# A two-layer encoder on one core: attention outputs moved to another pool, one distance table, and a written order for TensorE in the mixer

## The chip, the cores and the metric

The kernel runs on one core of one Trainium2 chip. The metric is the device time of one execution in microseconds (us); the kernel before takes 1097.06 us, the median of 3 runs (1096.51 to 1097.66).

## What is computed

Two layers, each of three sub-layers on 256 tokens of 1024 channels: a SwiGLU FFN with 2816 hidden channels, a token mixer, and a second FFN. Every sub-layer normalises its input, scales and shifts it by numbers from a conditioning vector, and adds its gated output to the residual. The mixer is the part that the change touches:

```
proj = n @ w_in                         # qa, ka, va, qd, kd, vd
qa = rope(rms(qa)); ka = rope(rms(ka))  # branch A: 8 query heads, 2 key heads
oa = softmax(qa @ ka.T / 8) @ va
sc = qd @ kd.T / 8 - slope[h] * |i - j| # branch B: 4 heads, two maps each
od = rms((softmax(sc[0]) - lam * softmax(sc[1])) @ vd)
g  = sigmoid(n @ w_gate + b_gate)
y  = (g_a * (oa @ w_ba) + g_b * (od @ w_bb)) @ w_o
```

The slopes of the four heads are 2^-2, 2^-4, 2^-6 and 2^-8.

## The kernel before, in words

All matrix products run on TensorE in float32r. An operand is split into a high part and the rest, and a product is three: high by high, rest by high, high by rest (mm3, lines 85 to 88). Weights come as 1 MB units through SP's queue into four raw buffers; ScalarE casts a half unit to its high part (whi, line 328) and VectorE subtracts it (wlo, line 330), each half into a slot of a pool of 23 slots of 4 KB per partition (w4). The same stream holds the units of the conditioning matrices, which VectorE reduces (raw<-raw,cb, line 245) or accumulates (gacc, line 276). pump makes the next halves; done calls it when a weight is used up.

The mixer's opening stretch, the front, goes from the end of the projection kv to the first gating product gt (lines 1026 to 1054). Its parts in the order of the code: to_T turns qr and kr of token half 0 (tt: four 128x128 transposes of qr, one of kr), proj_T makes half of qd's products (48, called pt), to_T turns token half 1, the other 48 of qd, a_scores(0, 0) (sc, 12 products), 48 products of kd, a_scores(0, 1), the other 48 of kd, a_T(0, 0) (8 transposes of softmax probabilities p, called pt as well, line 875), 24 products for vd (pj), a_T(0, 1), a_scores(1, 0), 24 more of vd, a_pv (ot) and a_scores(1, 1). kr is made from the projection by a reduction (hms), a power on GpSimd (hr), the rotation (q) and a product with hr, on VectorE (lines 757 to 826). p is made by a maximum on VectorE (nmx), two exponentials on ScalarE (line 852), a reciprocal (rs) and a product: by ScalarE for key head 0 (line 864), by VectorE for key head 1 (line 866).

The code's order is not the engines' order: a scheduler places the instructions of each engine within the dependencies, and only where follow ties two instructions is their order fixed. So TensorE's order in the front differs from the code's, as shown below.

After the front come the gates gt, branch B's attention, and merge: the products of the branches' outputs oaH, oaL, odH, odL with w_ba and w_bb (yb, 48 in each of four calls), whose moving operand is the branch output, 256 columns. The branch outputs lie in slots of w4, at 128 modulo 256 bytes; the modulated input nh and nl, which is the moving operand of gate and up products (g, u), qd, kd and gt, lies at 64 modulo 256, through a 192-byte tile ahead of it. In the FFN the last product of a down step, 512 columns wide, is parted in 264 and 248 columns (down_mm's part) ahead of the gate and up products.

Of the kernel before, what the change touches and what calls it, by code (L numbers as in the profile page):

```python
# [19 lines left out]
P = 128  # L20
# [22 lines left out]
def trunk(tc, a):  # L43
    nc = tc.nc
    with (
# [38 lines left out]

        def mm3(out, Lh, Ll, Rh, Rl, start, stop):
            nc.tensor.matmul(out, Lh, Rh, start=start, stop=False, skip_group_check=True)  # L86
            nc.tensor.matmul(out, Ll, Rh, start=False, stop=False, skip_group_check=True)  # L87
            nc.tensor.matmul(out, Lh, Rl, start=False, stop=stop, skip_group_check=True)  # L88
# [26 lines left out]
        for hf in range(2):  # L115
            x = slice(hf * 512, (hf + 1) * 512)
            bank = gen("cb")
            cmm = nc.tensor.matmul(bank, ones[0:1, :], crow[hf], start=True, stop=True)
            cact = nc.scalar.activation(cb[:, x], bank, AF.Silu)
# [169 lines left out]
        def gate_bcast(l, s):  # L289
# [5 lines left out]
            for hf in range(2):  # L295
# [5 lines left out]
                nc.tensor.matmul(bank, onesr, gh, start=True, stop=False, skip_group_check=True)  # L301
                nc.tensor.matmul(bank, onesr, gl, start=False, stop=True, skip_group_check=True)
# [57 lines left out]
        class Norm:  # L360
# [37 lines left out]
            def transposes(self):  # L398
                self.banks = []
                for hf in range(2):  # L400
                    bank = gen("nt")
                    for i in range(4):
                        nc.tensor.transpose(bank[:, i * P:(i + 1) * P], self.xs[hf][:, i * P:(i + 1) * P], ident)
# [82 lines left out]
        HF = [slice(0, 512), slice(512, 1024)]  # L486


        def new_hT():
            return (op.tile([P, 2, S], F32R, tag="hh", bufs=3, name=nm("hh")),  # L490
                    op.tile([P, 2, S], F32R, tag="hl", bufs=3, name=nm("hl")))

        def tok_hi(bank, ncol, unit_of, nT, t):
# [4 lines left out]
            for k in range(NK):  # L498
# [3 lines left out]
                nc.tensor.matmul(bank, nh[:, k, tok], wh[:, x], start=k == 0, stop=False, skip_group_check=True)  # L502
                nc.tensor.matmul(bank, nh[:, k, tok], wl[:, x], start=False, stop=False, skip_group_check=True)

        def tok_lo(bank, ncol, unit_of, nT, t, last):
            nh, nl = nT
            tok = slice(t * P, (t + 1) * P)
            for k in range(NK):
                u, i, c = unit_of(k)
                wh, wl = half(u, i)  # L510
                nc.tensor.matmul(bank, nl[:, k, tok], wh[:, c:c + ncol], start=False, stop=k == NK - 1, skip_group_check=True)
# [37 lines left out]
        def first_T(hts):  # L549

            tb = gen("tb")
            for t in range(2):
                for c in range(2):
                    nc.tensor.transpose(tb[:, c * 256 + t * P:c * 256 + (t + 1) * P], hts[t][:, c * P:(c + 1) * P], ident)
# [6 lines left out]
        def ffn(i, nT, norm1, first, nT_next):  # L561
# [6 lines left out]
            def down_mm(idx, t, hf, last, y=slice(0, 512), part=False):  # L568
# [4 lines left out]
                for c in range(2):  # L573
                    x = slice(c * 512 + y.start, c * 512 + y.stop)
                    if part and c == 1:

                        for L, R in ((hh, wh), (hl, wh)):
                            nc.tensor.matmul(acc[t][hf], L[:, c, tok], R[:, x], start=False, stop=False, skip_group_check=True)
# [827 lines left out]
```

## Time and profile before

| | |
|---|---|
| median of 3 runs | 1097.06 us |
| the profiled execution | 1097.68 us |
| its span, first to last instruction | 1095.9 us |
| TensorE busy in the span | 1082.9 us, 99% |
| VectorE busy | 864.9 us, 79% |
| ScalarE busy | 593.1 us, 54% |

The span leaves out 1.78 us that lie around it. A matmul's duration in the profile overlaps the next one's, so the rate of a stretch is read as its length by its number of products. In the views PE is TensorE, DVE VectorE, ACT ScalarE, POOL GpSimd; the timeline gives start and duration of merged rows, the windows give busy time of each engine in a stretch.

### The profile page before, as it was taken

The page shows a single profiled execution, that of the slowest core. Times are in us where ns is not written, and L with a number is a line of the kernel's source. Part 1 is how long each engine was busy: PE and PEld are TensorE (multiplying, and loading weights), DVE is VectorE, ACT ScalarE, POOL GpSimd, SP SyncE. Part 2 cuts the span into 40 slices and gives each one's busy share as a digit, 9 for nine tenths or more (in the row PEclk, how much of TensorE's full clock was granted, in tenths as well). Part 3 has the DMA queues.
Part 4 walks back from the last instruction along what each step waited for, and adds up shares of the span by engine and source line. Part 5 has one row for each costly group of instructions (what it writes and reads, how often), then busy time and mean ns, then how long its engine had stood idle before and what let it go on. Part 6 is the DMA issues. An engine that isn't in the chain of part 4 may idle for free.

```text
span 1095.9 us, 19235 instructions
## 1 busy us (share of the span) xinstructions
PE 1082.9 (99%) x7796; PEld 998.8 (91%) x7796; DVE 864.9 (79%) x1388; ACT 593.1 (54%) x916; POOL 44.5 (4%) x52
## 2 busy tenths in 40 slices
PE   8999999999999999999999999999999999999997
PEld 6989999898999899999989999989889998999996
DVE  5998986899978798886589886569988779766543
ACT  5564483558664554535455545435776547444432
POOL 1000000220010000000000000004000000000000
PEclk9999999999999999999999999999999999999999
DMA  8998996368745299997449987543865454876501
GB/s 315 380 368 336 380 335 219 120 263 332 264 172 193 86 376 357 347 377 266 150 152 357 365 288 285 202 165 126 297 236 189 157 190 183 315 267 229 197 19 39
DMA packets 44889, 271.12 MB, mean 247 GB/s; under 512 B 5880, under 2 KB 6648, under 8 KB 14848
## 3 DMA queue, kind: packets, MB, share of 16 engines
q1 hardware_dynamic: 42340, 267.93, 66.1%
q10 hardware_dynamic: 2460, 1.96, 0.6%
q8 instruction: 61, 1.00, 0.3%
q14 instruction: 28, 0.23, 0.1%
HBM read 268.82 MB, written 1.05 MB: 246 GB/s over the span
## 4 chain that ended last, share of the span: by engine, by line
PE 94%; DVE 3%; ACT 1%; issue 1%; POOL 0%; POOLq 0%
PE dn L87 6%; PE dn L88 6%; PE dn L86 6%; PE u L86 6%; PE g L86 6%; PE u L87 6%; PE g L88 6%; PE g L87 6%; PE u L88 6%; PE gt L86 3%; PE gt L88 3%; PE gt L87 3%; PE g L1199 2%; PE u L1199 2%; PE yb L88 1%; PE yb L87 1%
## 5 line engine op out<-in xcount | busy, mean ns | idle before, releaser
L330 DVE TENSOR_TENSOR wlo<-raw,whi 128x1024 fp32r<-128x1024 f32 x364 | 436.9, 1220 | 133.7 <-PE u L87 44.6
L328 ACT CAST whi<-raw 128x1024 fp32r<-128x1024 f32 x364 | 374.0, 1052 | 226.4 <-PE u L88 83.7
L86 PE MATMUL u<-nh,whi 128*128 128x256 f32 x592 | 164.0, 277 | 0.0
L86 PE MATMUL g<-nh,whi 128*128 128x256 f32 x592 | 164.0, 277 | 0.0
L87 PE MATMUL u<-nh,wlo 128*128 128x256 f32 x592 | 163.7, 277 | 0.0
L88 PE MATMUL g<-nl,whi 128*128 128x256 f32 x592 | 163.7, 277 | 0.0
L87 PE MATMUL g<-nh,wlo 128*128 128x256 f32 x592 | 163.7, 277 | 0.0
L88 PE MATMUL u<-nl,whi 128*128 128x256 f32 x592 | 163.6, 276 | 0.0
L86 PE MATMUL dn<-whi,hh 128*128 128x512 f32 (+1 forms) x326 | 126.0, 387 | 0.0
L87 PE MATMUL dn<-whi,hl 128*128 128x512 f32 (+1 forms) x326 | 125.9, 386 | 0.0
L88 PE MATMUL dn<-wlo,hh 128*128 128x512 f32 (+1 forms) x326 | 125.8, 386 | 0.0
L86 PEld LDWEIGHTS g<-nh,whi 128*128 128x128 f32 x592 | 111.2, 188 | 0.3
L87 PEld LDWEIGHTS g<-nh,wlo 128*128 128x128 f32 x592 | 111.2, 188 | 0.2
L86 PEld LDWEIGHTS u<-nh,whi 128*128 128x128 f32 x592 | 111.2, 188 | 0.1
L87 PEld LDWEIGHTS u<-nh,wlo 128*128 128x128 f32 x592 | 111.3, 188 | 0.0
L88 PEld LDWEIGHTS u<-nl,whi 128*128 128x128 f32 x592 | 111.2, 188 | 0.2
L88 PEld LDWEIGHTS g<-nl,whi 128*128 128x128 f32 x592 | 111.2, 188 | 0.0
L245 DVE CUSTOM_DVE_ANT_0 raw<-raw,cb 128x1024 f32<-128x1024 f32 x80 | 95.5, 1217 | 1.1 <-DMA raw<-in_ada_t_dram 0.9
L86 PE MATMUL gt<-nh,whi 128*128 128x256 f32 x256 | 73.7, 288 | 0.0
L88 PEld LDWEIGHTS dn<-wlo,hh 128*128 128x128 f32 x326 | 61.2, 188 | 12.4
L87 PEld LDWEIGHTS dn<-whi,hl 128*128 128x128 f32 x326 | 61.3, 188 | 11.1 <-DVE hl L546 0.2
L86 PEld LDWEIGHTS dn<-whi,hh 128*128 128x128 f32 x326 | 61.3, 188 | 11.1
(227 smaller groups left out, 2051.9 us busy)
## 6 DMA issues: line engine op xcount, KB each, us to landing
raw<-in_w_gu_dram SPq DMA_DIRECT2D x79, 1024.0 KB, 5.5
raw<-in_w_d_dram SPq DMA_DIRECT2D x41, 1024.0 KB, 6.4
raw<-in_ada_t_dram SPq DMA_DIRECT2D x40, 1024.0 KB, 6.8
raw<-in_ada_g_dram SPq DMA_DIRECT2D x24, 1024.0 KB, 6.3
raw<-in_w_in_dram SPq DMA_DIRECT2D x16, 1024.0 KB, 5.0
raw<-in_w_gate_dram SPq DMA_DIRECT2D x16, 1024.0 KB, 4.9
raw<-in_ada_t_dram SPq DMA_DIRECT2D x16, 512.0 KB, 6.5
raw<-in_w_gu_dram SPq DMA_DIRECT2D x32, 256.0 KB, 6.1
```

The source lines that it names most:

```text
L86: nc.tensor.matmul(out, Lh, Rh, start=start, stop=False, skip_group_check=True)
L87: nc.tensor.matmul(out, Ll, Rh, start=False, stop=False, skip_group_check=True)
L88: nc.tensor.matmul(out, Lh, Rl, start=False, stop=stop, skip_group_check=True)
L245: queue("dve", nc.vector.tensor_tensor_reduce(r, r, cb, 1.0, 0.0, op0=ALU.mult, op1=ALU.add, accum_out=col[:, k:k + 1]))
L328: split[1] = nc.scalar.copy(hi, r)
L330: split[0] = nc.vector.tensor_tensor(lo, r, hi.bitcast(F32), op=ALU.subtract)
L1199: nc.tensor.matmul(bank[:, c * 256:(c + 1) * 256], W[:, w], N[:, k, :], start=x + y + k + c == 0, stop=y == 1 and k == NK - 1, skip_group_ ...
```

## The change

The branch outputs leave w4: they share four buffers of 1088 words with the FFN's split activations, which now lie both in one such buffer, and begin 48 words into it, which is 64 modulo 256 bytes. w4 keeps its 23 slots. Branch B's query is scaled by 1/8 divided by its head's slope when it is split, so that one table of negative distances serves all heads, and the exponential multiplies by the slope. The last product ahead of the first yb (gb) and ahead of the third merge's yb (wo) is parted in 264 and 248 columns. Last, every TensorE instruction goes through an object that ties it to the one before while it is on: it is on from the first to_T of the mixer to the end of the last merge, so TensorE runs the code's order there.

```diff
+        class Ordered:
+            on, last = False, None
+            def then(self, ins):
+                if self.on and self.last is not None:
+                    follow(ins, self.last)
+                self.last = ins
+                return ins
+            def matmul(self, *args, **kw):
+                return self.then(nc.tensor.matmul(*args, **kw))
+            def transpose(self, *args, **kw):
+                return self.then(nc.tensor.transpose(*args, **kw))
+        pe = Ordered()
...
-                nc.tensor.matmul(bank, onesr, gl, start=False, stop=True, skip_group_check=True)
+                for z in (slice(0, PART), slice(PART, 512)) if part and hf else (slice(0, 512),):
+                    pe.matmul(bank[:, z], onesr, gl[:, z], start=False, stop=True, skip_group_check=True)
...
         def new_hT():
-            return (op.tile([P, 2, S], F32R, tag="hh", bufs=3, name=nm("hh")),
-                    op.tile([P, 2, S], F32R, tag="hl", bufs=3, name=nm("hl")))
+            x = op.tile([P, 1088], F32R, tag="h", bufs=4, name=nm("hhl"))
+            return tuple(x[:, i * 512:(i + 1) * 512].rearrange("p (c x) -> p c x", c=2) for i in range(2))
...
-                mc["pen"] = const("pen", [P, 4, 2, S])
+                mc["pen"] = const("pen", [P, 2, S])
+                nc.scalar.mul(mc["pen"], d, -1.0)
...
+                        if name == "qd":
+                            for x in range(2):
+                                o = [d[:, 2 * b + x, :] for d in dst]
+                                f = mc["qs"][:, x:x + 1]
+                                nc.scalar.activation(o[0], v[:, x, :], AF.Identity, scale=f)
+                                nc.vector.scalar_tensor_tensor(o[1], v[:, x, :], f, o[0].bitcast(F32), op0=ALU.mult,
+                                                               op1=ALU.subtract)
+                            continue
...
+            def branch_out(name):
+                x = op.tile([P, 1088], F32R, tag="h", bufs=4, name=nm(name))
+                return x[:, 48:48 + 4 * S].rearrange("p (k x) -> p k x", k=4)
...
-                    st["oa"] = (slot("oaH", (P, 4, S), F32R), slot("oaL", (P, 4, S), F32R))
+                    st["oa"] = (branch_out("oaH"), branch_out("oaL"))
...
-                        nc.scalar.activation(x[:, y], x[:, y], AF.Exp, bias=bi[:, m:m + 1], scale=0.125, accum_out=sm[:, m:m + 1])
+                        nc.scalar.activation(x[:, y], x[:, y], AF.Exp, bias=bi[:, m:m + 1], scale=SLOPES[2 * pair + e], accum_out=sm[:, m:m + 1])
...
             st["qaT"] = pair("qaT")
+            pe.on = True
             to_T(st["qr"][0], st["qaT"], 0, 4)
...
-            gate_bcast(l, 1)
+            gate_bcast(l, 1, True)
...
+                    if part and i == 1:
+                        for L, R in ((0, wh), (1, wh)):
+                            pe.matmul(acc[t][hf], ms_[k][:, L, tok], R[:, x], start=False, stop=False, skip_group_check=True)
+                        for z in (slice(0, PART), slice(PART, 512)):
+                            pe.matmul(acc[t][hf][:, z], ms_[k][:, 0, tok], wl[:, 512 + z.start:512 + z.stop], start=False,
+                                             stop=False, skip_group_check=True)
+                        continue
...
-                wo(0, 1, hf, 2)
+                wo(0, 1, hf, 2, hf == 1)
             merge(2)
             merge(3)
-            free(4)
+            pe.on = False
```

TensorE at the start of layer 0's front, around the transpose of the first kr (tt is the bank it goes to, ident the identity, pt the bank of qd's products). Before:

```order
L87 MATMUL pt_2537<-nh_164,wlo_2432 128x256
L88 MATMUL pt_2537<-nl_165,whi_2431 128x256
L86 MATMUL pt_2537<-nh_164,whi_2431 128x256
L87 MATMUL pt_2537<-nh_164,wlo_2432 128x256
L787 MATMUL tt_2532<-ident,kr_2466 128x128
L88 MATMUL pt_2537<-nl_165,whi_2431 128x256
L86 MATMUL pt_2536<-nh_164,whi_2431 128x256
```

Now, at the same place:

```order
L97 MATMUL kv_2460<-whi_2134,nl_165 128x256 x4
L97 MATMUL kv_2460<-whi_2247,nl_165 128x256 x4
L100 MATMUL tt_2516<-ident,qr_2398 128x128 x4
L100 MATMUL tt_2523<-ident,kr_2457 128x128
L97 MATMUL pt_2527<-nh_164,whi_2290 128x256
L97 MATMUL pt_2527<-nh_164,wlo_2291 128x256
```

The transpose of kr stood behind 35 of qd's products and stands now ahead of all 96. The second kr stood behind 105 products and stands behind 48.

VectorE in the same stretch, where the second kr is made (q is the rotation, gacc a unit of the stream). Before:

```order
L762 TENSOR_REDUCE hms_2602<-hsq_2600 128x2
L774 TENSOR_TENSOR q_431_2607<-kv_2469,ropec_1726 128x128
L779 TENSOR_TENSOR q_432_2609<-kv_2469,ropes_1727 128x4x16 x2
L791 TENSOR_TENSOR qaT_2524<-tt_2617,qaT_2523 128x4x128
L820 TENSOR_TENSOR q_431_2607<-q_431_2607,q_432_2609 128x128
L276 SCALAR_TENSOR_TENSOR gacc_2115<-raw_2495,ccol,gacc_2115 128x1024
L825 TENSOR_SCALAR kr_2614<-q_431_2607,hr_2605 128x64 x2
```

Now:

```order
L793 TENSOR_REDUCE hms_2593<-hsq_2591 128x2
L805 TENSOR_TENSOR q_420_2598<-kv_2460,ropec_1720 128x128
L810 TENSOR_TENSOR q_421_2600<-kv_2460,ropes_1721 128x4x16 x2
L295 SCALAR_TENSOR_TENSOR gacc_2107<-raw_2486,ccol,gacc_2107 128x1024
L856 TENSOR_TENSOR q_420_2598<-q_420_2598,q_421_2600 128x128
L295 SCALAR_TENSOR_TENSOR gacc_2107<-raw_2486,ccol,gacc_2107 128x1024
L861 TENSOR_SCALAR kr_2605<-q_420_2598,hr_2596 128x64 x2
```

Both halves of the gacc unit now stand ahead of kr and the split of qaT behind it. In layer 1, and in layer 0 up to the first kr, VectorE's rows stand as before.

TensorE later in layer 0's front, at a_T(0, 0) (p are the probabilities: p_2709 and p_2717 of token half 0 for key heads 0 and 1, p_2811 and p_2819 of token half 1). Now:

```order
L97 MATMUL pt_2722<-nl_165,whi_2585 128x256
L100 MATMUL pt_2906<-ident,p_2709 128x128 x2
L100 MATMUL pt_2906<-ident,p_2811 128x128 x2
L100 MATMUL pt_2913<-ident,p_2717 128x128 x2
L100 MATMUL pt_2913<-ident,p_2819 128x128 x2
L97 MATMUL pj_2920<-whi_2671,nh_164 128x512
```

Before, only the transposes of token half 0 stood there, and those of token half 1 behind the 24 products of vd's first half:

```order
L88 MATMUL pt_2727<-nl_165,whi_2594 128x256
L875 MATMUL pt_2911<-ident,p_2714 128x128 x2
L875 MATMUL pt_2918<-ident,p_2722 128x128 x2
L502 MATMUL pj_2925<-whi_2680,nh_164 128x512
L503 MATMUL pj_2925<-wlo_2681,nh_164 128x512
```

## Rows read from the trace of the kernel before

**Rows 1.** The page's parts 1 and 4: busy time, and the chain.

```profile
PE 1082.9 (99%) x7796; PEld 998.8 (91%) x7796; DVE 864.9 (79%) x1388; ACT 593.1 (54%) x916; POOL 44.5 (4%) x52
...
PE 94%; DVE 3%; ACT 1%; issue 1%; POOL 0%; POOLq 0%
```

**Rows 2.** Windows, TensorE alone: stretch, length, busy (instructions), granted clock, DMA.

```profile
324.10:335.62 11.52, 11.52 (x98) 1.00 0.42 148
415.82:426.73 10.91, 10.91 (x99) 1.00 1.01 380
22.72:62.18 39.46, 39.46 (x337) 1.00 1.02 382
```

**Rows 3.** Windows, both fronts: length, busy of PE, PEld, DVE, ACT, POOL.

```profile
219.98:264.25 44.27, 44.21 (x333) 39.12 (x331) 42.92 (x85) 31.26 (x63) 7.23 (x8) 1.00 0.76 278
756.66:799.61 42.95, 42.71 (x333) 37.93 (x331) 39.95 (x83) 30.73 (x62) 5.36 (x6) 1.00 0.77 276
```

**Rows 4.** Windows, TensorE: unbroken blocks of gt (48), sc, pj (24), ot, transposes (8).

```profile
264.25:269.88 5.63, 5.63 (x50) 1.00 0.97 381
239.49:240.39 0.90, 0.90 (x13) 1.00 0.96 401
748.45:753.94 5.49, 5.49 (x26) 1.00 0.12 16
261.47:263.35 1.88, 1.88 (x17) 1.00 0.62 214
251.89:252.69 0.80, 0.80 (x10) 1.00 1.01 348
```

**Rows 5.** Timeline of TensorE, transposes of qr and kr: start, duration, instruction.

```profile
219.98 0.60 PE L787 MATMUL tt<-ident,qr 128*128 128x128 f32 x4
220.33 0.37 PE L86 MATMUL pt<-nh,whi 128*128 128x256 f32 x1
...
224.40 0.27 PE L787 MATMUL tt<-ident,kr 128*128 128x128 f32 x1
...
756.66 0.60 PE L787 MATMUL tt<-ident,qr 128*128 128x128 f32 x4
```

**Rows 6.** Timeline of VectorE in both fronts; in brackets the idle time before.

```profile
217.60 2.36 DVE L330 TENSOR_TENSOR wlo<-raw,whi 128x1024 fp32r<-128x1024 f32 x2
219.88 0.28 DVE L762 TENSOR_REDUCE hms<-hsq 128x2 f32<-128x128 f32 x1
...
223.71 0.42 DVE L825 TENSOR_SCALAR kr<-q,hr 128x64 f32<-128x64 f32 x2 [0.63 <-POOL hr L124]
...
231.02 1.28 DVE L276 SCALAR_TENSOR_TENSOR gacc<-raw,ccol,gacc 128x1024 f32<-128x1024 f32 x1
232.21 0.41 DVE L825 TENSOR_SCALAR kr<-q,hr 128x64 f32<-128x64 f32 x2
...
758.76 0.41 DVE L825 TENSOR_SCALAR kr<-q,hr 128x64 f32<-128x64 f32 x2
...
768.35 0.41 DVE L825 TENSOR_SCALAR kr<-q,hr 128x64 f32<-128x64 f32 x2
```

**Rows 7.** Groups by line and form: count, busy, mean ns, idle before.

```profile
L245 DVE CUSTOM_DVE_ANT_0 raw<-raw,cb 128x1024 f32<-128x1024 f32 x80 | 95.5, 1217 | 1.1 <-DMA raw<-in_ada_t_dram 0.9
L844 DVE TENSOR_REDUCE nmx<-sc 128x2 f32<-128x512 f32 x16 | 10.9, 682 | 2.2 <-PE sc L840 2.2
L934 DVE SCALAR_TENSOR_TENSOR xb<-xb,rs 128x256 f32<-128x256 f32 x16 | 7.5, 481 | 0.2
L750 DVE TENSOR_TENSOR qd<-pt,qd 128x512 fp32r<-128x512 f32 x4 | 2.6, 678 | 0.0
L864 ACT ACTIVATE p<-p,rs 128x256 f32<-128x256 f32 x16 | 7.3, 505 | 0.8 <-DVE rs L860 0.8
L866 DVE TENSOR_SCALAR p<-p,rs 128x256 f32<-128x256 f32 x16 | 4.9, 347 | 0.0
L749 ACT CAST kd<-pt 128x512 fp32r<-128x512 f32 x4 | 2.2, 590 | 0.0
```

**Rows 8.** Windows, TensorE, end of the program: length, busy, granted clock.

```profile
1088.00:1093.90 5.90, 0.96 (x9) 1.00 0.14 52
1094.00:1095.90 1.90, 0.00 (x0) 0.50 0.24 93
```

More of the change, by code (lines that the diff above doesn't have):

```diff
@@ L117, in trunk @@
             bank = gen("cb")
-            cmm = nc.tensor.matmul(bank, ones[0:1, :], crow[hf], start=True, stop=True)
+            cmm = pe.matmul(bank, ones[0:1, :], crow[hf], start=True, stop=True)
             cact = nc.scalar.activation(cb[:, x], bank, AF.Silu)
@@ L287, in gate_start, with gate_bcast @@
             nc.scalar.dma_start(m["gacc"][0:1, :], a["ada_b_row"][l, s:s + 1, :])
-        def gate_bcast(l, s):
+        def gate_bcast(l, s, part=False):
             m = mods[(l, s)]
@@ L402, in transposes @@
                     for i in range(4):
-                        nc.tensor.transpose(bank[:, i * P:(i + 1) * P], self.xs[hf][:, i * P:(i + 1) * P], ident)
+                        pe.transpose(bank[:, i * P:(i + 1) * P], self.xs[hf][:, i * P:(i + 1) * P], ident)
                     self.banks.append(bank)
@@ L553, in first_T @@
                 for c in range(2):
-                    nc.tensor.transpose(tb[:, c * 256 + t * P:c * 256 + (t + 1) * P], hts[t][:, c * P:(c + 1) * P], ident)
+                    pe.transpose(tb[:, c * 256 + t * P:c * 256 + (t + 1) * P], hts[t][:, c * P:(c + 1) * P], ident)
             tv = tb.rearrange("p (c x) -> p c x", c=2)
@@ L786, in to_T @@
                 for i in range(n):
-                    nc.tensor.transpose(bank[:, i * P:(i + 1) * P], src[:, i * P:(i + 1) * P], ident)
+                    pe.transpose(bank[:, i * P:(i + 1) * P], src[:, i * P:(i + 1) * P], ident)
                 tok = slice(t * P, (t + 1) * P)
@@ L839, in a_scores @@
                             pr = slice(v * 64, (v + 1) * 64)
-                            nc.tensor.matmul(banks[v][:, i * 256:(i + 1) * 256], st["qaT"][x][pr, 2 * jj + i, tok], kaT[y][pr, 0, :],
+                            pe.matmul(banks[v][:, i * 256:(i + 1) * 256], st["qaT"][x][pr, 2 * jj + i, tok], kaT[y][pr, 0, :],
                                              start=x + y == 0, stop=y == 1, skip_group_check=True)
@@ L874, in a_T @@
                         for c in range(2):
-                            nc.tensor.transpose(bank[:, c * 256 + t * P:c * 256 + (t + 1) * P],
+                            pe.transpose(bank[:, c * 256 + t * P:c * 256 + (t + 1) * P],
                                                 probs[jj, v, t][:, i * 256 + c * P:i * 256 + (c + 1) * P], ident)
@@ L939, in b_T @@
                     for c in range(2):
-                        nc.tensor.transpose(bank[:, c * 256 + t * P:c * 256 + (t + 1) * P], xs[hd, t][0][:, c * P:(c + 1) * P], ident)
+                        pe.transpose(bank[:, c * 256 + t * P:c * 256 + (t + 1) * P], xs[hd, t][0][:, c * P:(c + 1) * P], ident)
                 if hd % 2 == 0:
@@ L972, in b_outT @@
                 for hd in range(4):
-                    nc.tensor.transpose(bank[:, hd * P:(hd + 1) * P], on[:, hd * P:(hd + 1) * P], ident)
+                    pe.transpose(bank[:, hd * P:(hd + 1) * P], on[:, hd * P:(hd + 1) * P], ident)
                 if t == 0:
-                    st["od"] = (slot("odH", (P, 4, S), F32R), slot("odL", (P, 4, S), F32R))
+                    st["od"] = (branch_out("odH"), branch_out("odL"))
                 nf = b2("onf")
@@ L1120, in mixer, with wo @@
             acc = []
-            def wo(u, t, hf, last):
+            def wo(u, t, hf, last, part=False):
                 if not acc:
@@ L1263, in keep_busy @@
             for _ in range(n):
-                ins = nc.tensor.matmul(bank.rearrange("p (r x) -> p r x", r=4), ident, ident4, start=True, stop=True)
+                ins = pe.matmul(bank.rearrange("p (r x) -> p r x", r=4), ident, ident4, start=True, stop=True)
                 follow(ins, first_)
@@ L1289, in turn @@
             for i in range(4):
-                tr = nc.tensor.transpose(nts[t, hf][:, i * P:(i + 1) * P], xs[:, i * P:(i + 1) * P], ident)
+                tr = pe.transpose(nts[t, hf][:, i * P:(i + 1) * P], xs[:, i * P:(i + 1) * P], ident)
             return tr
```

34 lines of the change are left out of this document (18 added, 16 removed).

## The prediction

> **What bounds the kernel now.** I read the busy times and the chain of waits first: TensorE is busy 1082.9 us of the 1095.9 us span, and 94% of the chain is TensorE [rows 1]. So only two things can move the time: TensorE's own rate somewhere, or a new stretch in which it has nothing to do. The span is 1.78 us short of the profiled execution (1097.68 us), which itself is 0.62 us above the median; I sum against 1097.68 and take 0.62 off at the end.
>
> Then the windows by stage. A yb call, 96 products (the two extra instructions in the row are its neighbours), takes 11.52 us, 120.0 ns a product. The gate and up stretch takes 10.91 us for the same 96, 113.6 ns. A long stretch of 336 without parted products takes 39.46 us, 117.4 ns [rows 2]. So yb runs slower than either kind of its like at the same granted clock of 1.00: some of its time is waste.
>
> Last, the two fronts, because the order of TensorE changes there. They take 44.27 and 42.95 us, TensorE is busy nearly all of it, and VectorE is busy 42.92 and 39.95 us of it [rows 3]. Two full engines side by side, each feeding the other: TensorE waits for VectorE's kr and p, VectorE for TensorE's banks. TensorE's lack of pauses rests on what stands between. The blocks show how little is wasted: 192 products for qd and kd are 4 x 5.63, 48 for vd 2 x 5.49, four sc 3.60, ot 1.88, two sets of 8 transposes 1.60 [rows 4], the transposes of qr and kr 2 x 0.35 (the distance from 219.98 to 220.33) and about 0.1 for each kr [rows 5], together 41.5 us. Layer 0 spends 2.8 us more than that, layer 1 1.4 us.
>
> **The change part by part.**
>
> *Branch outputs at 64 modulo 256, and parted products ahead of yb.* Same products, same columns, another address of the moving operand, which is then that of the gate and up products. Four stretches of 96 products (two merges of two halves per layer, so 384). If they come to the gate and up rate they gain 4 x (11.52 - 10.91) = 2.44 us; if only the address works and the parting doesn't, they come to 117.4 ns, a gain of 384 x 2.6 ns = 1.0 us; if neither, nothing. No row excludes that address or parting makes it worse, but the nearest rows at the new address are both faster, so I bound it at 0 to -2.44 and take **-2.4**. The parting itself adds four instructions of the same total columns; bound 0 to 4 x 0.114 us, I take 0, since the parted gate and up stretch shows none.
>
> *Distances, slopes, qd.* The split of qd is a cast on ScalarE and a subtraction on VectorE, 128x512, two pairs per layer; they become four pairs of 128x256. A 128x512 subtraction is 0.678 us; a VectorE scalar-tensor-tensor of 128x256 is 0.481 us [rows 7], less some 0.08 that each overlaps the next: 2 x 0.40 for 0.60, so +0.2 us of VectorE for each old pair, 0.4 us per layer. On ScalarE a scaled copy of 128x256 is bounded by the 0.505 of p's product and the 0.590 of a 128x512 cast [rows 7]: up to 0.5 us more for each old pair, hidden, as ScalarE is busy 31 of 44 us [rows 3]. VectorE's 0.4 us lie in its full queue and are counted in the replay below. Three fewer penalty tables and the slope in the exponential's scale change no instruction on the path: 0.
>
> *The pool of w4.* 23 slots stay, of which four no longer go to branch outputs: the stream may run further ahead behind a merge. TensorE waits for no weight there now [rows 1, 2], so 0; its cover is TensorE itself.
>
> *The written order.* This is the term that decides. I replayed the new order of every engine by the durations of the rows.
>
> Layer 0. qr's transposes end at 220.33. Before, 35 products stood between them and kr's transpose at 224.40 [rows 5], which kr allowed: VectorE starts kr at 223.71 and needs 0.42 us, after a 0.63 us wait for GpSimd's power [rows 6]. Nothing in VectorE's order ahead of it moves, so kr is ready at 224.13 as before, and TensorE, whose next instruction is now the transpose, stands for **3.8 us** with 96 ready products behind it. Then 48 products (5.63, to 229.9), qr's second transposes (to 230.2) and the second kr: VectorE starts it at 232.21 now; the split of qaT (0.60) falls behind it, one more half of gacc (1.19, from 231.02 to 232.21) comes ahead, so it starts at 232.8 and ends at 233.2 [rows 6]. Pause **3.0 us**. Then products and scores without a wait: 48, sc, 48, sc, 48 = 3 x 5.63 + 2 x 0.90, to 252.0.
>
> Now a_T(0, 0) wants p of both token halves. VectorE's queue between the second kr and that p: two splits of qaT and kaT, to 234.0; then six wlo at 1.14, two gacc at 1.19 [rows 6] and four reductions of raw at 1.14 (1.217 less the overlap), four nmx at 0.60, four half splits of qd at 0.40, two p at 0.27 [rows 7] and some seven small rows at under 0.08: 6.84 + 2.38 + 4.56 + 2.40 + 1.60 + 0.54 + 0.55 = 18.9, to 252.9. Behind it ScalarE finishes two casts of kd (0.5 each, the 0.590 less an overlap) and the product p (0.5) [rows 7]: 254.4. Pause **2.4 us**. It is the softest of the terms: 0 if ScalarE and VectorE get ahead by what TensorE stands (VectorE waits for products now and then too), 4 if the second kr's delay comes through in full. Behind that, 24 products for vd give VectorE room. Front: 41.5 + 3.8 + 3.0 + 2.4 = 50.7 and some 0.2 us of smaller waits, 50.9 against 44.27: **+6.6**.
>
> Layer 1. qr's transposes end at 757.0; kr is made from 758.76 to 759.17 [rows 6]: pause **2.15**. 48 products to 764.9, qr to 765.2; the second kr now starts at 768.35 [rows 6] and ends at 768.76, its place in VectorE's order unchanged: **3.6**. At a_T(0, 0) the same sum for VectorE ends about 0.2 us behind TensorE. Front: 41.5 + 2.15 + 3.6 + 0.2 = 47.4 against 42.95: **+4.4**.
>
> What goes away against this: the 2.8 and 1.4 us of small waits of the old fronts, already in these numbers. Sum: 6.6 + 4.4 - 2.4 = **+8.6**, so 1106.3, and less 0.62, **1105.7**. The four pauses at kr alone are 12.6 us against 4.2 us of old waste, so with no pause at a_T and yb at its best the floor of this mechanism is +12.6 - 4.2 - 2.4 = +6.0, or 1103; with a yb that doesn't move and 4 us at a_T it is 1109.8.
>
> **A rule on the clock.** In this trace the granted clock is 1.00 wherever TensorE works; it falls to 0.50 only at the very end: the last products lie before 1094, in a stretch that holds 0.96 us of work in 5.90, and at 1094 the row shows 0.50 [rows 8]. Of the two levels, 2.4 and 1.2 GHz, that is the lower. The new pauses of 2 to 3.8 us lie below that, and above any that the trace shows inside a stage.
>
> The Trainium skill, page "TensorE: Matmul & The Clock Gate", section "Why this matters for your kernels", advises against idle gaps between bursts of matmuls because the clock goes back to its lower level; by that the first pause in layer 0 would be followed by slow products, by my row it is not decided. It makes the second rival below.
>
> **The rivals.**
>
> *VectorE sets the front's end anyway (faster).* VectorE is busy 42.92 of 44.27 us in layer 0's front [rows 3]. If TensorE's pauses only bring forward the waits that it would have had, the front ends where VectorE's queue ends it, about as now, with fewer broken blocks: and yb's -2.4. The point from which it decides: the pauses at kr must sum to less than 4.2 + 2.4 = 6.6 us instead of 12.6, with none at a_T, so kr must come 1.5 us earlier at each of its four places. At 2.6 us earlier they sum to 2.2, and the time is 1097.06 + 2.2 - 4.2 - 2.4 = 1092.7. For it: kr rests on GpSimd's power, which moves, and VectorE's fullness. Against it: VectorE's order ahead of three of the four kr is unchanged, and nothing there waits for TensorE; and TensorE's own busy share is 44.21 of 44.27, so its work isn't slack.
>
> *The clock falls in a pause (slower still).* After a long pause 48 products would run at 1.2 GHz: 5.63 us more for each such fall. Some of it hides later waits (the 2.4 at a_T). One fall: 1105.7 + 5.6 = 1111.3, two: 1116.9. For it the rule above; against it that the one fall in the trace follows a longer rest.
>
> *The changes cancel.* If the pauses at kr are half of what I read (2 x 3.15 less) and a_T's is gone, 6.3 - 4.2 - 2.4 leaves -0.3: 1096.8, no change. It needs kr 1.5 us earlier on average; only GpSimd's 0.63 us [rows 6] is seen to vary.
>
> *yb doesn't move.* TensorE's rate there may be set by something other than address and parting: 1105.7 + 2.4 = 1108.1; with the address alone, 1107.1.
>
> **How the numbers follow.** About 0.2% (2.2 us) is what a measurement of this kernel can tell from no change. The written order costing some 6 to 13 us with yb improved or not: 0.77. The clock falling: 0.12. The cancelling case: 0.05. VectorE as bound: 0.06. So faster 0.06, same 0.05, slower 0.89. Range: from 1101 (the floor of 1103 less 2 for kr's moving earlier with GpSimd's and ScalarE's work) to 1112.5 (one fall of the clock, and a us of yb's gain missing).
>
> **What would show it.** In the profile after: idle time of TensorE ahead of the four rows that transpose kr, released by VectorE's kr, of about 3.8, 3.0, 2.15 and 3.6 us, in layer 0 also one ahead of the transposes of p; fronts of some 50.9 and 47.4 us; yb calls of 10.9 us; a granted clock of 1.00 throughout. It is wrong if those rows show no idle time or VectorE's kr starts more than a microsecond earlier than now; if the clock shows 0.5 behind a pause, the second rival holds.

## The result and the profile after

The changed kernel takes 1116.09 us (median of 4 runs), the kernel before 1097.36 in the same runs: a ratio of 1.0169, 95% interval 1.0152 to 1.0187. The forecast was 1105.7 in a range from 1101 to 1112.5. The direction was right, the loss was more than twice what was forecast (18.7 against 8.6 us), and the time lies outside the range.

The page of the kernel after, its parts 1 and 4 (busy time, and the chain of waits by engine), answers to [rows 1]:

```profile
PE 1083.5 (97%) x7800; PEld 997.4 (90%) x7800; DVE 866.4 (78%) x1392; ACT 589.4 (53%) x917; POOL 45.2 (4%) x56
...
PE 80%; DVE 11%; ACT 3%; issue 2%; DMA 1%; POOL 1%; POOLq 0%; SPq 0%; DVEq 0%; ACTq 0%
```

TensorE's busy time has hardly moved (1082.9 to 1083.5 us), while the span grew from 1095.9 to 1113.7. The loss is idle TensorE, and the chain's TensorE share falls from 94 to 80%: 11% is now VectorE's.

Where it lies is told by windows over the same stretches of both kernels. Those of before from the first gt to the first yb, both layers (columns: stretch, length, then busy time and instructions of PE, PEld, DVE, ACT, POOL, granted clock, DMA share, GB/s):

```profile
264.25:324.10 59.85, 59.85 (x527) 57.58 (x525) 54.84 (x146) 41.75 (x91) 2.85 (x3) 1.00 0.68 252
799.61:859.46 59.85, 59.85 (x527) 57.59 (x525) 51.48 (x135) 41.77 (x91) 2.85 (x3) 1.00 0.56 199
```

And after: both fronts (against [rows 3]), both stretches from gt to yb, and the four yb stretches of 96 products, below called yb calls (against [rows 2]):

```profile
219.57:272.37 52.80, 45.62 (x332) 40.52 (x330) 45.06 (x87) 31.71 (x65) 7.71 (x8) 0.94 0.69 251
766.41:815.10 48.69, 42.67 (x333) 37.88 (x331) 40.92 (x85) 31.12 (x64) 5.18 (x6) 1.00 0.66 243
272.37:334.92 62.55, 60.77 (x528) 57.66 (x526) 56.24 (x148) 43.18 (x94) 2.30 (x3) 1.00 0.65 236
815.10:877.59 62.49, 60.75 (x527) 57.64 (x526) 53.83 (x137) 43.32 (x94) 2.02 (x2) 1.00 0.54 200
334.92:345.81 10.89, 10.89 (x98) 10.89 (x97) 6.93 (x11) 3.22 (x5) 0.67 (x1) 1.00 0.37 135
351.27:362.18 10.91, 10.91 (x99) 10.91 (x97) 7.41 (x11) 2.62 (x4) 0.00 (x0) 1.00 0.52 194
877.59:888.90 11.31, 11.31 (x98) 11.31 (x97) 6.94 (x11) 3.24 (x6) 0.95 (x1) 1.00 0.38 143
894.39:905.30 10.91, 10.91 (x99) 10.91 (x97) 7.41 (x11) 2.62 (x4) 0.00 (x0) 1.00 0.52 187
```

The fronts lose 52.80 - 44.27 = 8.5 and 48.69 - 42.95 = 5.7 us. The gates lose 62.55 - 59.85 = 2.7 and 62.49 - 59.85 = 2.6, where the forecast had no term at all. The four yb stretches gain 4 x 11.52 - 44.02 = 2.1. That is 17.5 of the span's 17.8; the rest lies in small pieces elsewhere.

TensorE's timeline, the rows that wait, layer 0 then layer 1 (start, duration, instruction; in brackets the idle time before it and who ended it):

```profile
223.73 0.33 PE L100 MATMUL tt<-ident,kr 128*128 128x128 f32 x1 [3.56 <-DVE kr L861]
...
232.92 0.30 PE L100 MATMUL tt<-ident,kr 128*128 128x128 f32 x1 [1.34 <-DVE kr L861]
...
254.21 1.17 PE L100 MATMUL pt<-ident,p 128*128 128x128 f32 x6 [2.27 <-ACT p L900]
...
768.79 0.33 PE L100 MATMUL tt<-ident,kr 128*128 128x128 f32 x1 [1.79 <-DVE kr L861]
...
778.47 0.30 PE L100 MATMUL tt<-ident,kr 128*128 128x128 f32 x1 [3.44 <-DVE msh L269]
...
798.49 0.87 PE L100 MATMUL pt<-ident,p 128*128 128x128 f32 x6 [0.80 <-ACT p L900]
```

All the pauses of the forecast are there. (msh, named at the second kr of layer 1, is the small row directly behind kr on VectorE.) Counted from the start of the last product before to the start of the waiting one, less one product, they are 3.7, 1.5 and 2.4 us in layer 0 (3.8, 3.0 and 2.4 were forecast) and 1.95, 3.6 and 1.0 in layer 1 (2.15, 3.6 and 0.2).

What was only a rival is there too: the granted clock falls behind two of them. A window of TensorE alone among the products behind the first pause, then windows over all 48 products that follow it and over the 24 products of vd behind p:

```profile
225.50:227.00 1.50, 1.50 (x9) 0.50 0.89 371
```

```profile
223.82:230.97 7.15, 7.15 (x49) 7.15 (x50) 7.15 (x15) 1.65 (x4) 3.65 (x5) 0.76 0.51 160
...
255.03:262.04 7.01, 7.01 (x27) 5.62 (x25) 2.38 (x4) 0.83 (x2) 0.00 (x0) 0.78 0.75 280
```

0.50 is the lower of the two levels, 1.2 GHz. The 48 products take 7.15 us instead of the 5.63 of [rows 4], and only their first part is slow; the 24 take 7.01, where [rows 4] has 5.49.

### The profile page after: what moved, and what is told of

It is laid out like the page before. It is cut to its first block, busy times and chain, and to the rows that moved or that the text cites. A ratio compares the mean times of both kernels' runs of the same rounds, so it can differ in the third digit from the quotient of the medians.

```text
span 1113.7 us, 19225 instructions
## 1 busy us (share of the span) xinstructions
PE 1083.5 (97%) x7800; PEld 997.4 (90%) x7800; DVE 866.4 (78%) x1392; ACT 589.4 (53%) x917; POOL 45.2 (4%) x56
## 4 chain that ended last, share of the span: by engine, by line
PE 80%; DVE 11%; ACT 3%; issue 2%; DMA 1%; POOL 1%; POOLq 0%; SPq 0%; DVEq 0%; ACTq 0%
PE dn L97 21%; PE g L97 19%; PE u L97 19%; PE yb L97 4%; PE wo L97 4%; PE gt L97 4%; DVE wlo L350 4%; PE gu L97 3%; PE pj L97 2%; PE pt L97 1%; ACT whi L348 1%; DVE raw L264 1%; PE nt L100 1%; DVE nf L446 1%; DMA raw<-in_ada_t_dram 1%
## 5 line engine op out<-in xcount | busy, mean ns | idle before, releaser
L97 PE MATMUL dn<-whi,hhl 128*128 128x512 f32 (+1 forms) x716 | 219.1, 387 | 0.1
L97 PE MATMUL g<-nh,whi 128*128 128x256 f32 x656 | 179.8, 278 | 0.9 <-ACT nh L1257 0.9
L97 PE MATMUL u<-nh,whi 128*128 128x256 f32 x656 | 179.1, 277 | 0.0
L97 PE MATMUL g<-nh,wlo 128*128 128x256 f32 x656 | 178.9, 277 | 0.1
L97 PE MATMUL u<-nh,wlo 128*128 128x256 f32 x656 | 178.8, 277 | 0.0
L97 PEld LDWEIGHTS dn<-whi,hhl 128*128 128x128 f32 x716 | 130.9, 188 | 24.9 <-DVE hhl L567 0.5
L97 PE MATMUL dn<-wlo,hhl 128*128 128x512 f32 (+3 forms) x390 | 138.4, 368 | 0.0
L97 PEld LDWEIGHTS dn<-wlo,hhl 128*128 128x128 f32 x390 | 73.3, 188 | 15.0
L97 PE MATMUL gt<-nl,whi 128*128 128x256 f32 x256 | 71.3, 279 | 0.0
L97 PE MATMUL gt<-nh,wlo 128*128 128x256 f32 x256 | 71.2, 278 | 0.0
```

The lines of the kernel that those rows point to most:

```text
L97: return self.then(nc.tensor.matmul(*args, **kw))
```

## The experiments

Each is an edit of the kernel after or before; the ratios are to the kernel before, in the same runs. "Front" and "gates" below are the two stretches of the windows above, layer 0 and layer 1.

### The other edits without the written order

```diff
-            pe.on = True
             to_T(st["qr"][0], st["qaT"], 0, 4)
...
-            pe.on = False
```

> The changed kernel without the written order: TensorE's instructions are placed by the scheduler again, everything else stays. Theory A (two causes: the written order costs only in the fronts, 8.5 us in layer 0 and 5.7 in layer 1, and the move of the branch outputs out of w4 costs 2.7 + 2.6 us at the end of the gates, where VectorE's and ScalarE's rows were reordered): the fronts come back to about 44.3 and 43.0 us, the stretch from the first gt to the first yb stays at 62.5 us, yb stays at 10.9, so about 1097.4 - 2.0 + 5.3 = 1100.7, some 15 us below the changed kernel. Theory B (the written order is the cause of all of it, the gates too): fronts and gates both come back, about 1095.3. Theory C (the halved splits of qd fill VectorE and lengthen the fronts): the fronts stay near 52 and 48 us, about 1116.

Measured: 1096.66 us, ratio 0.9988 (0.9979 to 0.9997). Its windows on TensorE, front and gates of both layers (length, busy, clock, DMA share, GB/s):

```profile
219.45:263.60 44.15, 44.15 (x333) 1.00 0.77 275
263.60:323.75 60.15, 60.15 (x525) 1.00 0.70 261
755.66:798.11 42.45, 42.45 (x332) 1.00 0.76 276
798.11:858.54 60.43, 60.43 (x526) 1.00 0.58 208
```

The halved splits of qd lengthen nothing (theory C falls: the fronts are 0.1 and 0.5 us shorter than before). For the gates neither A nor B is right as put: they lost 0.3 and 0.6 us instead of 2.7 or nothing. In the trace 16 products of the first yb stand ahead of gb's last ones here: the scheduler drew ready work into the hole. So the hole was still there, and the next runs had to find what makes it. Part of it moved past the end of this window: gb's last products now stand inside yb, and the first yb runs at 117.8 ns a product.

### The written order alone

The kernel before with the object that orders TensorE, on over the same stretch; branch outputs in w4, four distance tables, whole splits of qd, no parting.

```diff
+            pe.on = True
             to_T(st["qr"][0], st["qaT"], 0, 4)
...
             merge(3)
             free(4)
+            pe.on = False
```

> The kernel before with the written order alone: branch outputs in w4, four distance tables, whole splits of qd, no parted products. Theory A: fronts near 52.8 and 48.7 us, gates at the old 59.85 us, yb at 11.52, so about 1097.4 + 14.3 = 1111.7. Theory B: the gates lengthen too, about 1117. Theory C: fronts near the old ones, about 1097.

Measured: 1119.33 us, ratio 1.0196 (1.0182 to 1.0209): about what the whole change costs or somewhat more (1.0169, 1.0152 to 1.0187; the intervals just overlap). The fronts take 53.58 and 55.60 us, the gates 61.70 and 59.83, yb 120 ns a product. Theory A's sum was 7.6 us short, mostly in layer 1's front, where p came 3.5 us late instead of 1.0, and 48 products and the 24 behind p ran at a lowered clock. That the written order by itself is enough for a loss of this size holds; that it costs a fixed amount does not. Layer 1's gates are as before; layer 0's are 1.9 us longer, at the second branch's scores (1.14 us of idle time) and od and not at gb, so the stall at gb isn't the written order's alone.

### Four slots of w4 held empty

```diff
             def branch_out(name):
                 x = op.tile([P, 1088], F32R, tag="h", bufs=4, name=nm(name))
+                h = slot("hold", (P, 1024))
+                nc.gpsimd.memset(h[:, 0:1], 0.0)
+                st.setdefault("hold", []).append(h)
...
             merge(3)
+            for h in st["hold"]:
+                nc.gpsimd.tensor_copy(h[:, 0:1], ms_[7][:, 0, 0:1].bitcast(F32))
+            free(4)
```

> The changed kernel with four w4 slots held empty from the branch outputs to the last merge (a one-column write on GpSimd at either end), as many as the branch outputs took before; the branch outputs stay in the other pool. It takes away the four free slots and nothing else. Theory A (the free slots let halves of weights be cast and split earlier, ahead of gl and the normalised outputs on VectorE and ScalarE, and TensorE waits for those): the waits at od, ont and gb vanish, first gt to first yb back to 59.9 us in both layers, about 1116.1 - 5.3 = 1110.8, the fronts as in the changed kernel. Theory B: gates as in the changed kernel, 1116.

Measured: 1110.06 us, ratio 1.0109 (1.0096 to 1.0123). Front and gates of layer 0, then of layer 1:

```profile
219.74:272.58 52.84, 45.62 (x332) 0.94 0.69 250
272.58:332.43 59.85, 59.85 (x527) 1.00 0.66 236
763.79:813.96 50.17, 44.94 (x333) 0.93 0.64 235
813.96:873.81 59.85, 59.85 (x528) 1.00 0.55 199
```

Gates 59.85 us in both layers, to the hundredth what they were before; all yb calls at 113.5 ns. Theory A. VectorE's timeline at the end of layer 0's gates shows how, first after, then with the slots held (gl is the lower part of the gate that gb sends to all rows; wlo is the stream):

```profile
331.51 0.68 DVE L319 TENSOR_TENSOR gl<-gacc,gh 128x512 fp32r<-128x512 f32 x1
332.11 1.22 DVE L350 TENSOR_TENSOR wlo<-raw,whi 128x1024 fp32r<-128x1024 f32 x1
333.24 0.68 DVE L1017 TENSOR_TENSOR odL<-onf,odH 128x512 fp32r<-128x512 f32 x1
333.85 0.68 DVE L319 TENSOR_TENSOR gl<-gacc,gh 128x512 fp32r<-128x512 f32 x1
```

```profile
330.19 1.28 DVE L319 TENSOR_TENSOR gl<-gacc,gh 128x512 fp32r<-128x512 f32 x2
331.40 0.68 DVE L1020 TENSOR_TENSOR odL<-onf,odH 128x512 fp32r<-128x512 f32 x1
```

With free slots a half of the stream (wlo) and odL stand between the two gl, and the second gl ends at 334.53 us. TensorE waits for it, in the kernel after:

```profile
334.58 0.50 PE L97 MATMUL gb<-gl,onesr 128*128 128x264 f32 x2 [0.94 <-DVE gl L319]
```

The three places that lose time there are od (2.23 us instead of 1.71), the second ont (1.31 instead of 0.36) and gb (2.15 instead of 0.95): 2.7 us together, all of layer 0's gates.

### The written order from the first gate on only

```diff
-            pe.on = True
             to_T(st["qr"][0], st["qaT"], 0, 4)
...
+            pe.on = True
             gate_mm(0, 0)
```

> The changed kernel with the written order from the first gt to the last merge only; the front is left to the scheduler, the four slots stay free. Theory A (the stall at the end of the gates needs both the free slots and the fixed order, and not the late front): fronts 44.2 and 42.5 us, gates 62.5 in both layers, so 1097.9 - 2 + 5.3 - 0.5 = 1100.7. Theory B (the gates lose time because VectorE comes late out of the longer front): gates near 60, about 1096.

Measured: 1102.12 us, ratio 1.0035 (1.0022 to 1.0049). Fronts 44.15 and 42.45, gates 62.50 and 64.03 us. Theory A: the fronts are short, and the gates still lose 2.7 and 4.2; layer 1's further 1.5 come with waits at p and at the second branch's scores (0.54 and 0.32 us of idle time). The stall comes from the free slots and the fixed order together, not from a late front.

### No written order, slots held

Both edits: the order left out, and the four slots held.

> The changed kernel without the written order and with four w4 slots held empty, as in the runs before each alone. Theory A (the stall at gb comes from the free slots, and the free order only hid most of it by drawing products of yb ahead of gb): gates 59.85 us instead of 60.15 and 60.43, yb's two pairs 27.3 instead of 27.9 us because the parted product stands directly ahead of yb again, so about 1.2 + 0.9 us below the run with the free order alone: 1094.6 where the kernel before takes 1097.9. Theory B (the free order alone takes away all that the slots cost): like the free order alone, 1096.7.

Measured: 1095.29 us, ratio 0.9977 (0.9968 to 0.9986): a little below the kernel before, by 2.7 us, just above the 2.2 that the prediction took as what can be told from no change. Windows of TensorE, front and gates of layer 0, then of layer 1:

```profile
220.02:264.17 44.15, 44.15 (x332) 1.00 0.76 276
264.17:324.02 59.85, 59.85 (x527) 1.00 0.70 254
755.39:797.84 42.45, 42.45 (x333) 1.00 0.80 278
797.84:857.69 59.85, 59.85 (x528) 1.00 0.54 198
```

With yb at 113.5 ns in all four calls, this is what the change holds of use: 0.6 us in the fronts and 2.5 in merges (28.49 to 27.26 us from the first yb to the end of the second, in each layer). From the first gt to the end of the second yb the layers take 87.11 us each here, and 88.05 and 88.32 in the run with the free order and free slots: the hole of that run costs 2.2 us in all, the slower yb included.

### Address and parting, each alone

The address alone is the kernel with held slots and whole products ahead of yb; the parting alone is the kernel after with the branch outputs back in w4 (the diff shows oa; od went back too), where the FFN's split activations also have their two old tiles again.

```diff
-            gate_bcast(l, 1, True)
+            gate_bcast(l, 1)
...
-                wo(0, 1, hf, 2, hf == 1)
+                wo(0, 1, hf, 2)
```

```diff
-                    st["oa"] = (branch_out("oaH"), branch_out("oaL"))
+                    st["oa"] = (slot("oaH", (P, 4, S), F32R), slot("oaL", (P, 4, S), F32R))
```

> The changed kernel with four slots held and the products ahead of yb whole again: the address of the branch outputs alone. If the address sets yb's rate and the parting the start: 117 to 118 ns a product in all four stretches of 96, 11.3 us instead of 10.9. If the parting does nothing: 113.6. If the address does nothing: 120.0.

> The changed kernel with the branch outputs back in w4, at 128 modulo 256, while the products ahead of yb stay parted. If the address is what slows yb: 120.0 ns a product in all four stretches, as in the kernel before. If the parting is: 113.6.

Measured: 1108.39 and 1112.77 us, single times without an interval. The yb calls of layer 0, address alone; then, parting alone, the gates of layer 0 and its first yb call (length, busy, clock, DMA share, GB/s):

```profile
329.89:340.79 10.90, 10.90 (x97) 1.00 0.42 153
346.25:357.55 11.30, 11.30 (x97) 1.00 0.63 215
```

```profile
271.26:331.11 59.85, 59.85 (x527) 1.00 0.65 235
331.11:342.63 11.52, 11.52 (x98) 1.00 0.45 153
```

The second yb call there takes 11.52 us too. The parting does nothing at the old address. At the new one the call behind wo takes 11.30 us with whole products ahead of it and 10.91 with a parted one; the call behind gb takes 10.90 either way. Layer 1 repeats both. So the address is worth 0.62 + 0.22 us a layer, the parting 0.39, at one of its two places. "Address" here is the whole move to the other pool: no run changes the offset within one pool, so that the 64 modulo 256 does it is not shown. The second run also bears on the slots: with the order written and the branch outputs filling four slots of w4 the gates take 59.85 us in both layers, without any slot held.

### TensorE kept busy in its pauses

```diff
+            FILL = [(31, 26, 21), (17, 31, 8)][l]
             def to_T(src, dst, t, n):
                 bank = gen("tt")
+                for _ in range(FILL[t] if n == 1 else 0):
+                    pe.transpose(bank[:, 0:P], ident, ident)
...
                     for t in range(2):
+                        for _ in range(FILL[2] if (jj, i, v, t) == (0, 0, 0, 1) else 0):
+                            pe.transpose(bank[:, P:2 * P], ident, ident)
```

> The changed kernel with transposes of the identity in TensorE's pauses in the fronts (31, 26 and 21 of them in layer 0; 17, 31 and 8 in layer 1, at 0.11 us each), written to columns that the waiting transpose overwrites: TensorE is kept busy while it waits, the waits themselves stay. VectorE's order differs in a few places (the second kr ahead of a split of qaT). If the granted clock of 0.50 behind the pauses comes from their idle time: the clock stays at 1.00, the first 48 products of layer 0 take 5.6 instead of 7.15 us, which the wait for the second kr takes back, since that kr doesn't come earlier; the 24 products behind the p of layer 0 take 5.6 instead of 7.0, which is kept: about 1116.1 - 1.8 = 1114.3. If the clock falls for another reason: 1116.

> The filler transposes in TensorE's pauses and the four held slots together, so that the end of the gates can't take back what the fronts gain. Theory A (the fall of the clock costs 1.5 us in layer 0's front, and the free slots took it back in the run with the fillers alone): fronts 51.3 and 49 us, gates 59.85, about 1.5 to 2.5 us below the run with held slots alone, 1108. Theory B (VectorE is late by the front, whatever TensorE's clock is, and the lost time comes back behind the front): front and gates of layer 0 together near 112.7 as with held slots alone, 1110.

Measured: 1116.70 us, ratio 1.0170 (1.0156 to 1.0184), where the kernel after has 1.0169; with held slots 1109.62, ratio 1.0103 (1.0086 to 1.0120), where held slots alone have 1.0109 (1.0096 to 1.0123). Front and gates of layer 0, with the fillers alone, and with fillers and held slots:

```profile
221.14:272.43 51.29, 50.97 (x411) 1.00 0.67 247
272.43:336.90 64.47, 61.32 (x527) 1.00 0.65 239
```

```profile
219.78:271.13 51.35, 50.98 (x410) 1.00 0.67 244
271.13:332.34 61.21, 60.55 (x527) 1.00 0.68 242
```

The clock stays at 1.00 and layer 0's front gains 1.5 us, as expected. Then the gates give it back: 64.47 instead of 62.55, and 61.21 instead of 59.85. Front and gates together are 115.8 against 115.4 us with free slots, and 112.6 against 112.7 with held ones. What decides is behind the front too: the p of the front's last scores starts on ScalarE 60.6 us after the front's start with the fillers (281.76), in the kernel after 60.4 (280.00). TensorE comes earlier, p doesn't. Theory B holds for layer 0; layer 1's front moved by +0.3 and -1.0 us in the two pairs, no clear reading. The fall of the clock is real, and in layer 0 these two pairs show no time that it costs in the end; for other orders no run isolates it.

### The transposes of kr behind the products, p's behind vd

With held slots, the code's order changed at three places, and the rows that make the second kr (post_kv) moved ahead of qd's first products:

```diff
             to_T(st["qr"][0], st["qaT"], 0, 4)
-            to_T(st["kr"][0], kaT, 0, 1)
             qd, kd = [], []
+            post_kv(1, kv[1])
             proj_T("qd", 0, qd)
-            post_kv(1, kv[1])
+            to_T(st["kr"][0], kaT, 0, 1)
             to_T(st["qr"][1], st["qaT"], 1, 4)
-            to_T(st["kr"][1], kaT, 1, 1)
             proj_T("qd", 1, qd)
+            to_T(st["kr"][1], kaT, 1, 1)
...
-            a_T(0, 0)
             vd0 = proj("vd", 0)
+            a_T(0, 0)
```

> The changed kernel with four slots held, and its written order changed at three places: each transpose of kr behind the 48 products of qd instead of ahead of them, and the transposes of p behind the 24 products of vd. Theory A (the written order costs in the front only because it asks for kr and p right away): TensorE waits about 1 us at the second kr in layer 0, at most 2 at p, the fronts take some 46 and 44 us, the granted clock stays at 1.00, about 1097.9 - 2.4 + 3 = 1098.5. Theory B (any fixed order waits for VectorE, which is full, by about as much): fronts above 50 and 47, 1107 or more.

Measured: 1103.79 us, ratio 1.0046 (1.0033 to 1.0059), fronts 49.35 and 45.65 us: between the two theories. The waits for kr are gone. In layer 0 TensorE waits 2.3 us for the second qr instead, 0.35 and 0.98 for the split of kaT, and none for p; the clock fell twice. In layer 1 it waits 0.64, 0.35 and 2.28 at the same places. VectorE has layer 0's second qr ready 8.3 us after the front's start here and in the kernel after; TensorE only comes to it earlier, since it no longer stands at the first kr.

### The written order from the scores on

With held slots, the order is on only from a_scores(0, 0), behind all transposes of qr and kr.

```diff
-            pe.on = True
             to_T(st["qr"][0], st["qaT"], 0, 4)
...
             proj_T("qd", 1, qd)
+            pe.on = True
             a_scores(0, 0)
```

> The changed kernel with four slots held and the written order from a_scores(0, 0) on, so that the scheduler places the transposes of qr and kr among qd's products and the rest of the front stays as written (sc directly behind the second kr, p's transposes ahead of vd's products). Theory A (the four waits for kr are what the written order costs, p's is small): fronts near 46 and 44.5 us, with a wait of 1 to 2.5 us at sc for the split of kaT, 1098. Theory B (VectorE, full, sets the front's end in this order, and a wait taken away at kr comes back at p or sc): fronts above 49 and 47, 1104 or more.

Measured: 1108.45 us, ratio 1.0096 (1.0081 to 1.0111). Theory B. Three of the four waits for kr are gone and the last is 0.56 us in layer 0, yet the fronts are 52.37 and 49.66 us against 52.84 and 50.17 with held slots alone. The wait is now at p (in layer 1 also at the split of kaT, 0.36 and 1.29 us). TensorE's timeline of layer 0 there, then the window over the 24 products behind it:

```profile
251.93 0.66 PE L100 MATMUL pt<-ident,p 128*128 128x128 f32 x4 [4.07 <-ACT p L903]
253.98 0.69 PE L100 MATMUL pt<-ident,p 128*128 128x128 f32 x2 [1.40 <-DVE p L905]
```

```profile
254.32:262.57 8.25, 8.25 (x26) 0.65 0.81 281
```

So layer 0's front kept its length for two reasons: VectorE's last p came only 1.6 us earlier after the front's start than in the kernel after, and the clock fell for longer behind it (8.25 us where the kernel after has 7.01).

### And p's transposes behind the first products of vd

The run above with one move more:

```diff
-            a_T(0, 0)
             vd0 = proj("vd", 0)
+            a_T(0, 0)
             a_T(0, 1)
```

> The run with the written order from a_scores(0, 0) on, with one more place changed: the transposes of p stand behind the first 24 products of vd instead of ahead of them. Theory A (in every order p of token half 1 comes from VectorE 33 to 35 us after the front's start, and what the written order costs is the 24 products that it puts behind p, 5.6 us or 8.2 at the lower clock, with TensorE idle ahead of them): TensorE comes to p at about its time, waits at most 1 us there, fronts near 45 and 44 us, 1108.5 - 7.4 - 5.7 = 1095.5 with the gates at 59.85. Theory B (VectorE sets the front's end wherever the products stand): the wait moves to the next p or sc, fronts above 49 and 47, 1103 or more.

Measured: 1098.25 us, ratio 1.0005 (0.9996 to 1.0014). Front and gates of layer 0, then the front of layer 1 (its gates take 59.85 us):

```profile
220.20:264.27 44.07, 42.81 (x333) 1.00 0.73 266
264.27:325.28 61.01, 60.55 (x527) 1.00 0.69 258
756.17:801.93 45.76, 44.11 (x333) 0.96 0.73 260
```

Theory A. One move of 24 products takes 8.3 us out of layer 0's front, 2.7 of them the slow clock behind p, and 3.9 out of layer 1's; the distance to the kernel before falls from 10.4 to 0.9 us. TensorE's wait for p is down to this:

```profile
253.65 1.31 PE L100 MATMUL pt<-ident,p 128*128 128x128 f32 x10 [0.19 <-DVE p L905]
```

It was 2.8 us more than expected: layer 0's gates took 61.01 us, and layer 1's front 45.76, where TensorE waits 0.35 and 1.29 us for the split of kaT, with a slow stretch behind.

## Why the prediction was wrong

**The bound and the ledger.** That only TensorE's rate or its idle time could move the time held: its busy time is the same to 0.6 us. By terms, forecast and measured in the profiled runs: layer 0's front +6.6 and +8.5, layer 1's +4.4 and +5.7, yb -2.4 and -2.1, gates 0 and +5.3. Of the 9.2 us that were missed in the span, more than half is the term at zero.

**The step that failed: "The pool of w4. 23 slots stay ... TensorE waits for no weight there now, so 0; its cover is TensorE itself."** I asked whether the stream would come sooner, not what it would push aside. Held slots gave back all 5.3 us, and so did the branch outputs back in w4. Free slots bring halves of the stream ahead of rows that TensorE needs, gl and the normalised outputs; VectorE is busy 51 to 55 of 60 us there. The prediction's part on the order of VectorE stopped at the front. And it needed the second edit: with a free order TensorE fills the hole with products of yb, and 0.9 of 5.3 us is left in the gates, 2.2 with what moved behind them. With the order as in the change and the slots held, nothing is lost. A second, smaller loss in layer 0's gates stays open: 1.9 us with the order alone, 1.4 with fillers and held slots, 1.2 in the last run, each with no free slot and with waits at p or at the second branch's scores.

**The fronts: sizes near, reason wrong.** Each pause was read from the rows nearly as it came (3.7 against 3.8, 2.4 against 2.4, 3.6 against 3.6), and the replay of VectorE's queue put layer 0's p 34.4 us after the front's start, where ScalarE's p ended TensorE's wait at 34.6 (254.17). But I named the four waits for kr as the certain price and p's as the softest term, and had it backwards. VectorE's last p of token half 1 ends 33.3 us after the front's start before, 35.3 in the kernel after, 33.7 with the order on from the scores; what changed is what stands behind it: 11.0 us of front before, 17.5 after, 18.7 in that run, 10.4 when the 24 products of vd stand ahead. VectorE's rows for it:

```profile
252.64 0.61 DVE L866 TENSOR_SCALAR p<-p,rs 128x256 f32<-128x256 f32 x2
```

```profile
254.51 0.34 DVE L902 TENSOR_SCALAR p<-p,rs 128x256 f32<-128x256 f32 x1
```

```profile
253.58 0.61 DVE L905 TENSOR_SCALAR p<-p,rs 128x256 f32<-128x256 f32 x2
```

They are those of before, of after, and with the order on from the scores. So the price of the written order in layer 0 is the 24 products that it puts behind p (5.5 us), 1.5 for their slow clock, less some 0.5 of small waits that went, and 2.0 by which p comes later. For layer 1 no such sum was made. The order rows ahead of the prediction show that move; I priced it only as a pause. The floor of +6.0, which counted the kr pauses alone, was no floor: without three of them and most of the fourth the fronts stayed, in layer 0 because p came only 1.6 us earlier and 1.2 of that went to a longer fall of the clock.

**The rival on the clock.** I gave the fall 0.12 and a price of 5.6 us, "one fall: 1111.3". It came twice in layer 0 and cost 1.5 us each time in place, the first taken back at the second kr (its pause 1.5 instead of 3.0). The price of 5.6 took a whole block at the lower rate; only part of each block was slow. That its sum for two falls, 1116.9, lies next to the measured 1116.09 is chance: two falls cost 3.0 us in place, not 11. The Trainium skill, page "TensorE: Matmul & The Clock Gate", section "Why this matters for your kernels", advises against idle gaps between bursts of matmuls because the clock drops back. The trace agrees that a gap within a stage can lower the clock (0.50 behind 3.56 us), but not that every such gap does (1.00 behind 3.44 us in layer 1). The runs with fillers show a gain of 1.5 us in layer 0's front, given back in the gates. There it explains the front's length, not the time.

**The rival "VectorE sets the front's end anyway"** had the right bound with the wrong sign: VectorE's p does set the pace, and because the order puts work behind it that had covered it, the end comes later. **yb**: the bound of -2.44 was nearly reached (-2.1; all of it with the slots held), but about two thirds is the address. **qd, distances, the slopes**: 0 held, by the first experiment.

## What to carry to other kernels

When a buffer pool gets room, look at what the freed work will displace on the engines that make it, not only at who waited for the room. A fixed order on the bounding engine takes away its means to fill holes, so its price is read at the operand that comes last from the full engine: count the ready work that the new order puts behind it, and move that ahead. Pauses before that point are not additive: without some 10 us of pauses at kr each of the two fronts was 0.5 us shorter.

## What was not expected of the hardware

The granted clock did not follow the length of a pause: 0.50 behind 3.56 us of idle time at the first kr of the kernel after, but 1.00 behind 3.60 us at the same place with the order alone, where it fell behind 2.94 us at the second kr (48 products in 5.55 and then 8.43 us). Nor did equal pauses agree: the second kr of layer 1 came behind 3.44 us in the kernel after (1.00) and in the run with held slots (0.50). The two rows with the order alone:

```profile
223.40:228.95 5.55, 5.55 (x49) 1.00 0.48 187
232.60:241.03 8.43, 8.43 (x49) 0.65 0.91 316
```

The rate of 128x256 products has three values here by address and by what stands ahead: 120.0, 117.8 and 113.5 ns. At the new address the first yb of a pair came out at 113.5 or 117.8 ns with the same instructions ahead of it: after a stall at gb it was 113.5 in layer 0 and 117.8 in layer 1 of the kernel after, the other way round with the order from the first gate on, and 113.4 in both with the fillers alone. What chooses between these two is open.
